# The second FFN product in 2x2 blocks: seven multiplications for sixteen of its twenty-two row tiles

## The chip, the cores and the metric

The kernel runs on one core of a Trainium2 chip. The core has a matrix engine (PE in the profile, its weight loads as PEld), a vector engine (DVE), an activation engine (ACT), a general-purpose engine (POOL), and a queue that only issues transfers (SP). Each works through a queue of its own in a fixed order; semaphores make one wait for another. The metric is device time of one execution in microseconds, the median of the runs.

## The reference

A decoder layer on 1024 tokens of width 1024: two kinds of attention, gates, an output projection, and then a SwiGLU FFN of inner width 2816 (22 row tiles of 128). All in float32. The part that changes is the last line but one:

```python
        h2 = rms_norm(x, norm_ffn_g[layer])
        gu = h2 @ w_ffn_in[layer]
        x = x + (jax.nn.silu(gu[..., :D_FF]) * gu[..., D_FF:]) @ w_ffn_down[layer]
    return rms_norm(x, norm_final_g)
```

Call `A` the 1024 x 2816 activation and `W` the 2816 x 1024 matrix `w_ffn_down`. The second product is `A @ W`, to which `x` (the residual) is added before the last norm.

## The kernel before, in words

Float32 products are made of three PE instructions each. `split` (L95 to L97) turns a float32 operand into a rounded part `hi` (a copy on ACT, L96) and the rest `lo` (a subtraction on DVE, L97: both inputs and the output lie in SBUF). `mm3` (L99 to L102) multiplies hi by hi, hi by lo and lo by hi into the same PSUM bank. One such instruction takes 128 rows of the left operand's 128 columns and 512 columns of the right one. There are six banks of the kind `pd` that this stage uses.

The first FFN product already runs in 2x2 blocks with seven multiplications: there `left_side` (L260 to L278) combines the weights' blocks on POOL (lines L272 to L277), and `up` (from L1013) makes 20 of the 22 row tiles of `A`, each of which POOL stores to `a_dram` (L1039).

The second product, which the change rewrites, is at the end. It walks over nine groups of row tiles (1, 1, 2, 3, 3, 2, 3, 3 and 4 of them). Of each row tile it loads 128 rows of `A` and 128 rows of `W` (`load_w`, L107 to L123; 512 KB each, issued by SP) and splits them. Then it goes through the eight token tiles and the two halves of the columns: one PSUM bank collects the group's products (3 per row tile), and DVE adds the bank to the accumulator `acc` in SBUF (L1080; in the first group ACT copies, L1078). In the fourth group POOL adds the residual to `acc` (L1086). In the last group each finished token tile is normed (L1081 to L1097) and stored by ACT and SP (L1099). Buffers for split rows are seven deep, so loads and splits run ahead of PE.

The order of the instructions in each engine's queue is made when the program is built: a scheduler goes by its own estimate of times. A place in a queue is fixed from then on.

Of the kernel before, what the change touches and what calls it, by code (L numbers as in the profile page):

```python
# [20 lines left out]
HALF = 512  # L21
# [9 lines left out]
NFF = DFF // P  # L31
# [16 lines left out]
def layer_kernel(  # L48
# [39 lines left out]
    def nm(s):  # L88
        uid[0] += 1
        return f"{s}_{uid[0]}"  # L90

    def pd():
        return psd.tile([P, HALF], F32, tag="d", name=nm("pd"))

    def split(hi, lo, src):  # L95
        nc.scalar.activation(out=hi, in_=src, func=AF.Copy)  # L96
        return nc.vector.tensor_tensor(out=lo, in0=src, in1=hi.bitcast(F32), op=ALU.subtract)  # L97

    def mm3(psum, w, m, start, stop):  # L99
        nc.tensor.matmul(psum, w.hi, m.hi, start=start, stop=False)  # L100
        nc.tensor.matmul(psum, w.hi, m.lo, start=False, stop=False)  # L101
        last_mm[0] = nc.tensor.matmul(psum, w.lo, m.hi, start=False, stop=stop)  # L102
# [31 lines left out]
    def load_gain(pool, g):  # L134
        t = pool.tile([P, D], F32, tag="gain", name=nm("gain"), bufs=1)
        nc.scalar.dma_start(out=t[:], in_=g.broadcast_to([P, D]))
        return t

# [243 lines left out]
    with pool_of("foxv", 2) as vpool:  # L382
# [31 lines left out]
        for i in range(NT):  # L414
            load_x()
            hh, c = divmod(i * P, HALF)
# [139 lines left out]
    fpool = f_ctx.__enter__()  # L556
# [286 lines left out]
    for i, (br, dt) in enumerate(merge_order):  # L843
        n = br * KT + dt
# [200 lines left out]
    h_ctx.__exit__(None, None, None)  # L1045


    groups, at = [], 0
    for n in (1, 1, 2, 3, 3, 2, 3, 3, 4):
        groups.append(list(range(at, at + n)))  # L1050
        at += n
    with pool_of("down", 1) as fpool:
        acc = fpool.tile([P, NT, D], F32, name="acc", bufs=1)
        for gi, grp in enumerate(groups):
            last = gi == len(groups) - 1
            if gi == 4:
                gainf = load_gain(fpool, norm_final_g.unsqueeze(0))
            ats, ws = [], []
            for j in grp:
                for to, src, tag in ((ats, a_dram[j], "at"), (ws, w_ffn_down[j * P:(j + 1) * P, :], "wd")):  # L1060
                    to.append(load_w(src, 1, D) if gi == 0 else
                              load_w(src, 1, D, tag=tag, bufs=7, pool=fpool, rbufs=2 if gi == 1 else 3,
                                     rpool=wpool if gi == 1 else fpool))
            for t in range(NT):
                sq = [None, None]
                if last:
                    xf = fpool.tile([P, D], F32, tag="xf", name=nm("xf"), bufs=3)
                if gi == 3:
                    xr = fpool.tile([P, D], F32, tag="xf", name=nm("xr"), bufs=3)
                    nc.gpsimd.dma_start(out=xr[:], in_=x1_dram[t])  # L1070
                for ch in range(2):
                    cs = slice(ch * HALF, (ch + 1) * HALF)
                    pt = pd()
                    for n in range(len(grp)):
                        mm3(pt[:], ats[n][:, 0, t * P:(t + 1) * P], ws[n][:, 0, cs],
                            n == 0, n == len(grp) - 1)
                    if gi == 0:
                        nc.scalar.activation(out=acc[:, t, cs], in_=pt[:], func=AF.Copy)  # L1078
                    else:
                        nc.vector.tensor_tensor(out=acc[:, t, cs], in0=pt[:], in1=acc[:, t, cs], op=ALU.add)  # L1080
                    if last:  # L1081
                        sq[ch] = small.tile([P, 1], F32, tag="sq", name=nm("sq"))
                        nc.scalar.activation(out=xf[:, cs], in_=acc[:, t, cs], func=AF.Square,
                                             accum_out=sq[ch][:])
                if gi == 3:
                    nc.gpsimd.tensor_tensor(out=acc[:, t], in0=acc[:, t], in1=xr[:], op=ALU.add)  # L1086
                if last:
                    ss = small.tile([P, 1], F32, tag="ss", name=nm("ss"))
                    nc.vector.tensor_tensor(out=ss[:], in0=sq[0][:], in1=sq[1][:], op=ALU.add)
                    nc.vector.tensor_tensor(out=xf[:], in0=acc[:, t, :], in1=gainf[:], op=ALU.mult)  # L1090
                    r = rstd(ss, True)
                    for ch in range(2):
                        cs = slice(ch * HALF, (ch + 1) * HALF)
                        if ch == 0:
                            nc.scalar.activation(out=xf[:, cs], in_=xf[:, cs], func=AF.Copy, scale=r[:, 0:1])
                        else:
                            nc.vector.tensor_scalar(out=xf[:, cs], in0=xf[:, cs], scalar1=r[:, 0:1],  # L1097
                                                    scalar2=None, op0=ALU.mult)
                        (nc.scalar, nc.sync)[ch].dma_start(out=out[t * P:(t + 1) * P, cs], in_=xf[:, cs])  # L1099


# [27 lines left out]
```

## Time and profile before

| what | value |
|---|---|
| median of three runs (lowest to highest) | 1507.62 us (1504.62 to 1509.13) |
| the profiled execution's own time | 1507.19 us |
| its span from first to last instruction | 1505.5 us |
| mean granted PE clock | 0.995 |
| PE busy over the span | 1463.1 us (97%) |
| first matmul of the second product | 1247.47 us |
| last matmul of the second product ends | 1497.45 us |
| matmuls of the second product | 1056 (22 row tiles x 16 banks x 3) |

Times in the views are microseconds from the span's start. A group's row gives how often, the busy time, the mean of one in ns, and the engine's idle time just before it with what ended it. A timeline's row gives start, length, engine, line, output<-inputs and shape. A busy PE share counts overlapping instructions, so the distance from one weight load to the next (PEld) is the better clock of PE's pace.

### The profile page before, as it was taken

The numbers are of one execution on the slowest core, as the hardware profiler recorded it, in microseconds if no ns is written. First come the engines' busy times: TensorE is split into PE (matmuls) and PEld (weight loads), VectorE is DVE, ScalarE is ACT, GpSimd is POOL, SyncE is SP. The second block draws the span as 40 slices with busy tenths as digits, with TensorE's granted clock in tenths as the row PEclk, the third lists the DMA queues.
The fourth block names the chain that finished last, engine by engine and source line by source line (L and its number), as shares of the span: only waits on it lengthen the run. The fifth ranks groups of instructions, "written<-read, shape, count | busy, mean of one in ns | idle before, by whom it ended". The sixth has DMA issues, their size and how long they took to land.

```text
span 1505.5 us, 18223 instructions
## 1 busy us (share of the span) xinstructions
PE 1463.1 (97%) x6920; PEld 1183.9 (79%) x6920; DVE 910.7 (60%) x1344; ACT 530.6 (35%) x808; POOL 440.8 (29%) x398
## 2 busy tenths in 40 slices
PE   6999999999999999999999999999999999999997
PEld 6898888886767666688888788888888877888886
DVE  6482654449888999736528944444444435856546
ACT  5242332226765332355215432222222225312113
POOL 1002434445443311100000245555555552240000
PEclk9999999999999999999999999999999999999999
DMA  8132454475453442175623132222222235643202
GB/s 253 43 105 70 137 165 124 137 202 122 131 137 117 141 165 71 52 238 168 227 64 133 42 91 66 82 84 84 84 84 84 84 99 197 205 144 90 93 14 98
DMA packets 148503, 177.91 MB, mean 118 GB/s; under 512 B 12096, under 2 KB 113472, under 8 KB 148416
## 3 DMA queue, kind: packets, MB, share of 16 engines
q1 hardware_dynamic: 115536, 97.56, 21.9%
q10 hardware_dynamic: 21264, 38.81, 8.1%
q0 software_dynamic: 11616, 40.39, 7.7%
q8 instruction: 54, 0.88, 0.2%
q14 instruction: 33, 0.27, 0.1%
HBM read 125.35 MB, written 51.38 MB: 117 GB/s over the span
## 4 chain that ended last, share of the span: by engine, by line
PE 84%; DVE 7%; DMA 3%; ACT 2%; issue 2%; POOL 2%; ACTq 0%; SPq 0%; DVEq 0%; POOLq 0%
PE pd L284 33%; PE pd L100 10%; PE pd L102 10%; PE pd L101 10%; PE pf L100 3%; PE pf L101 3%; PE pf L102 3%; PE pd L190 2%; PE pd L194 2%; PE pd L191 2%; PE pd L664 2%; PE pd L613 1%; PE pd L614 1%; DMA wr<-in_w_in_dram 1%; DVE mx L766 1%
## 5 line engine op out<-in xcount | busy, mean ns | idle before, releaser
L284 PE MATMUL pd<-hT_t,wh 128*128 128x512 f32 x856 | 264.4, 390 | 1.5 <-ACT cc L310 0.8
L96 ACT ACTIVATE wh<-wr 128x1024 fp32r<-128x1024 f32 (+2 forms) x152 | 139.4, 923 | 316.5 <-PE pd L101 88.8
L97 DVE TENSOR_TENSOR wl<-wr,wh 128x1024 fp32r<-128x1024 f32 (+2 forms) x152 | 164.3, 1084 | 132.3 <-ACT wh L96 132.0
L284 PE MATMUL pd<-tT,wh 128*128 128x512 f32 x768 | 236.3, 389 | 2.2 <-DVE v L952 1.1
L284 PEld LDWEIGHTS pd<-hT_t,wh 128*128 128x128 f32 x856 | 160.5, 188 | 35.3 <-ACT cc L310 1.2
L284 PEld LDWEIGHTS pd<-tT,wh 128*128 128x128 f32 x768 | 144.0, 188 | 32.9 <-DVE v L952 1.6
L284 PE MATMUL pd<-hT_t,wl 128*128 128x512 f32 x428 | 168.0, 393 | 0.2 <-DVE wl L97 0.2
L272 POOL TENSOR_TENSOR s<-wr 128x512 f32<-128x512 f32 x29 | 41.3, 1426 | 371.5 <-DVE tT L97 203.2
L284 PE MATMUL pd<-tT,wl 128*128 128x512 f32 x384 | 148.5, 390 | 0.1
L100 PE MATMUL pd<-wh,wh 128*128 128x512 f32 x352 | 137.3, 391 | 3.4 <-DVE acc L1080 2.0
L101 PE MATMUL pd<-wl,wh 128*128 128x512 f32 x352 | 137.0, 389 | 0.0
L102 PE MATMUL pd<-wh,wl 128*128 128x512 f32 x352 | 137.0, 389 | 0.0
L1080 DVE TENSOR_TENSOR acc<-pd,acc 128x512 f32<-128x512 f32 x128 | 85.4, 686 | 66.9 <-PE pd L102 66.8
L97 DVE TENSOR_TENSOR wl<-s,wh 128x1024 fp32r<-128x1024 f32 x58 | 73.8, 1274 | 68.8 <-ACT wh L96 68.8
L100 PE MATMUL pf<-hT_t,wh 128*128 128x512 f32 x288 | 114.3, 397 | 0.4 <-ACT wh L96 0.4
L101 PE MATMUL pf<-hT_t,wh 128*128 128x512 f32 x288 | 114.2, 397 | 0.0
L102 PE MATMUL pf<-hT_t,wl 128*128 128x512 f32 x288 | 113.6, 395 | 0.0
L96 ACT ACTIVATE wh<-s 128x1024 fp32r<-128x1024 f32 x58 | 61.4, 1060 | 132.3 <-POOL s L273 103.2
L284 PEld LDWEIGHTS pd<-hT_t,wl 128*128 128x128 f32 x428 | 80.3, 188 | 21.7 <-DVE wl L97 5.4
L284 PEld LDWEIGHTS pd<-tT,wl 128*128 128x128 f32 x384 | 72.1, 188 | 15.4 <-DVE wl L97 0.5
L100 PEld LDWEIGHTS pd<-wh,wh 128*128 128x128 f32 x352 | 66.1, 188 | 19.6 <-DVE acc L1080 2.9
L102 PE MATMUL pd<-wh,hT_t 128*128 128x512 f32 (+1 forms) x208 | 79.1, 382 | 0.0
(251 smaller groups left out, 2756.1 us busy)
## 6 DMA issues: line engine op xcount, KB each, us to landing
wr<-in_w_in_dram SPq DMA_DIRECT2D x46, 512.0 KB, 4.7
wr<-in_w_ffn_in_dram SPq DMA_DIRECT2D x44, 512.0 KB, 4.2
wr<-a_dram SPq DMA_DIRECT2D x22, 512.0 KB, 4.2
wr<-in_w_ffn_down_dram SPq DMA_DIRECT2D x22, 512.0 KB, 4.0
a_dram<-a POOLq DMA_DIRECT2D x20, 512.0 KB, 5.1
g_dram<-fst ACTq DMA_DIRECT2D x32, 256.0 KB, 2.3
land<-g_dram SPq DMA_DIRECT2D x16, 512.0 KB, 3.4
dqk_dram<-qo POOLq DMA_DIRECT2D x20, 256.0 KB, 3.7
```

Source lines behind the costliest of these rows:

```text
L96: nc.scalar.activation(out=hi, in_=src, func=AF.Copy)
L97: return nc.vector.tensor_tensor(out=lo, in0=src, in1=hi.bitcast(F32), op=ALU.subtract)
L100: nc.tensor.matmul(psum, w.hi, m.hi, start=start, stop=False)
L101: nc.tensor.matmul(psum, w.hi, m.lo, start=False, stop=False)
L102: last_mm[0] = nc.tensor.matmul(psum, w.lo, m.hi, start=False, stop=stop)
L190: nc.tensor.matmul(pt[hh][:], w.hi[:, k], m.hi, start=(k == 0), stop=False)
L191: nc.tensor.matmul(pt[hh][:], w.hi[:, k], m.lo, start=False, stop=False)
L194: nc.tensor.matmul(pt[hh][:], w.lo[:, k], m.hi, start=False, stop=(k == kt - 1))
L272: nc.gpsimd.tensor_tensor(out=s12[:, :4], in0=u1, in1=u2, op=ALU.add)
L284: last_mm[0] = nc.tensor.matmul(bank[:], p, q, start=first and k == 0 and n == 0, stop=k == 3 and n == 2, skip_group_check=True)
L664: nc.tensor.matmul(po[half[e], HALF - width[j]:], vf[j // 4][:, j % 4, pr, e], L[:, off[j]:off[j + 1]], start=(j == nj - 1), stop=(j == 0) ...
L1080: nc.vector.tensor_tensor(out=acc[:, t, cs], in0=pt[:], in1=acc[:, t, cs], op=ALU.add)
```

## The change

Row tiles 0, 1 and 2 are now done one by one as before (`PLAIN_UP`), and 19, 20 and 21 together at the end (`LAST`), where the norm is. The sixteen between are three chunks of 4, 6 and 6 row tiles. In a chunk of `2c` row tiles, `A`'s part is cut into four blocks (first or second half of the tokens, first or second `c` row tiles) and `W`'s part likewise (row tiles by halves of the columns). `block` makes seven products of such blocks instead of eight: four banks each, `c` row tiles deep, 12c matmuls. A chunk takes 84c matmuls where it took 96c.

The price is combined operands. Eight sums or differences of blocks per chunk (`comb`) run on POOL, each over 128 x (c*512) elements with both inputs in SBUF. Every product splits both of its operands anew (`product`): 14 splits of 128 x (c*512) per chunk, each a copy on ACT and a subtraction on DVE, where a chunk had 4c splits of 128 x 1024 before. Two partial sums belong to three quarters of the result: they are kept apart in `shared` over all chunks (`keep`), and only in the last chunk POOL adds them (`share`, four additions of 128 x 2048). The residual comes in the second chunk, in eight additions of 128 x 1024 on POOL. The raw rows of a chunk lie in four of five buffers of one tag; the temporaries `s1`, `s2`, `t1`, `t2` have one buffer each, and `gainf` now shares `t2`'s. In the last rows the multiplication by the gain is on POOL for token tiles 0 to 5. When a bank is added to `acc`, `acc` is now the first input and the bank the second.

```diff
-    for n in (1, 1, 2, 3, 3, 2, 3, 3, 4):
+    PLAIN_UP = ((0,), (1,), (2,))
+    CHUNKS = (range(3, 7), range(7, 13), range(13, 19))
+    LAST = range(19, NFF)
+    CM = max(len(c) for c in CHUNKS) // 2
...
+        shared = [fpool.tile([P, NT // 2, HALF], F32, name=nm("shared"), bufs=1) for _ in range(2)]
+        def op():
+            return fpool.tile([P, CM, HALF], F32R, tag="op", name=nm("op"), bufs=8)
+        def raw_rows():
+            return fpool.tile([P, CM, S], F32, tag="raw", name=nm("raw"), bufs=5)
...
+        def add(out, bank, op=ALU.add):
+            nc.vector.tensor_tensor(out=out, in0=out, in1=bank[:], op=op)
...
+            def comb(out, p, q, op=ALU.subtract):
+                nc.gpsimd.tensor_tensor(out=out, in0=p, in1=q, op=op)
+                return out
+            def product(p, q, banks):
+                ops = []
+                for src in (p, q):
+                    hi, lo = op()[:, :c], op()[:, :c]
+                    split(hi, lo, src)
+                    ops.append(Pair(hi, lo))
+                l, r = ops
+                new = banks is None
+                banks = banks or [pd() for _ in range(NT // 2)]
+                for t, bank in enumerate(banks):
+                    ts = slice(t * P, (t + 1) * P)
+                    for n in range(c):
+                        for k, (x_, y_) in enumerate(((l.hi, r.hi), (l.hi, r.lo), (l.lo, r.hi))):
+                            nc.tensor.matmul(bank[:], x_[:, n, ts], y_[:, n], start=new and n == 0 and k == 0,
+                                             stop=n == c - 1 and k == 2, skip_group_check=True)
+                return banks
...
+            banks = product(a11, b11, None)
+            keep(0, banks)
+            banks = product(a12, b21, banks)
+            into(0, 0, banks)
+            s1, s2, t1, t2 = [tmp(n) for n in ("s1", "s2", "t1", "t2")]
+            comb(s1, a21, a22, ALU.add)
+            comb(s2, s1, a11)
+            comb(t1, b12, b11)
+            comb(t2, b22, t1)
+            banks = product(s2, t2, None)
+            into(0, 1, banks, residual=False)
+            banks = product(comb(a21, a11, a21), comb(b12, b22, b12), banks)
+            keep(1, banks)
+            banks = product(s1, t1, None)
+            into(H, 1, banks)
+            banks = product(comb(a12, a12, s2), b22, banks)
+            into(0, 1, banks)
+            if last:
+                share(acc[:, :H, HALF:], 0)
+                share(shared[0][:], 1)
+                share(acc[:, H:, HALF:], 0)
+            banks = product(a22, comb(b21, t2, b21), None)
+            into(H, 0, banks, ALU.subtract)
+            if last:
+                share(acc[:, H:, :HALF], 0)
```

How the queues now stand, at three places. First POOL in the second product. Before, its only work there was the residual:

```order
L1086 TENSOR_TENSOR acc<-acc,xr_10007 128x1024
L1086 TENSOR_TENSOR acc<-acc,xr_10032 128x1024
L1070 DMA xr_10082<-x_dram 128x1024
L1070 DMA xr_10107<-x_dram 128x1024
L1086 TENSOR_TENSOR acc<-acc,xr_10057 128x1024
```

Now, at the third chunk (L1122 is `comb`, L1158 the residual of the second chunk, L1157 its load):

```order
L1122 TENSOR_TENSOR s_1601_10724<-s_1600_10723,raw_10607 128x1536
L1122 TENSOR_TENSOR raw_10607<-raw_10607 128x3x512
L1158 TENSOR_TENSOR acc<-acc,xr_10487 128x2x512
L1158 TENSOR_TENSOR acc<-acc,xr_10490 128x2x512
L1157 DMA xr_10542<-x_dram 128x2x512
L1157 DMA xr_10545<-x_dram 128x2x512
L1122 TENSOR_TENSOR t_1603_10726<-raw_10619,t_1602_10725 128x1536
L1122 TENSOR_TENSOR raw_10611<-raw_10619,raw_10611 128x3x512
L1158 TENSOR_TENSOR acc<-acc,xr_10542 128x2x512
L1158 TENSOR_TENSOR acc<-acc,xr_10545 128x2x512
L1122 TENSOR_TENSOR raw_10615<-raw_10615,s_1601_10724 128x3x512
```

Six of the eight residual additions have thus moved in among the third chunk's combinations. The chunks' combinations stand eight in a row before that (second chunk), and the four additions of `share` and the six gain multiplications (L1209) stand in a row behind.

Second, DVE at one product of the second chunk (L97 is a split's subtraction, L1099 the addition of a bank):

```order
L97 TENSOR_TENSOR op_10388<-raw_10203,op_10387 128x1536
L1099 TENSOR_TENSOR acc<-acc,pd_10341 128x512
L97 TENSOR_TENSOR op_10392<-raw_10207,op_10391 128x1536
L1099 TENSOR_TENSOR acc<-acc,pd_10342 128x512
L1099 TENSOR_TENSOR acc<-acc,pd_10343 128x512
L1099 TENSOR_TENSOR acc<-acc,pd_10344 128x512
```

Every product has this pattern: one split, one bank, one split, three banks. Before, DVE had up to thirteen banks in a row between two splits.

Third, ACT at the third chunk (L96 is a split's copy, L136 the load of the last norm's gain):

```order
L96 ACTIVATE op_10735<-t_1603_10726 128x1536
L136 DMA gain_10991<-in_norm_final_g_dram 128x1024
L96 ACTIVATE op_10785<-raw_10607 128x1536
L96 ACTIVATE op_10789<-raw_10611 128x1536
```

The gain's load waits until POOL has read `t2` for the last time (the chunk's last combination), and the copies for the fourth product now stand behind it.

More of the change, by code (lines that the diff above doesn't have):

```diff
@@ new lines, in rows, with whole @@
+        def rows(j):
+            return a_dram[j], w_ffn_down[j * P:(j + 1) * P, :]
+        def whole(j, own):
+            if own:
+                return [load_w(src, 1, D)[:, 0] for src in rows(j)]
+            raw, both = raw_rows(), []
+            for i, src in enumerate(rows(j)):
+                load(raw[:, i], src)
+                hi, lo = [t[:].rearrange("p a c -> p (a c)")[:, :S] for t in (op(), op())]
+                split(hi, lo, raw[:, i])
+                both.append(Pair(hi, lo))
+            return both
@@ L1071, in layer_kernel, with plain_rows @@
+        def plain_rows(js, own, evac):
+            both = [whole(j, i == own) for i, j in enumerate(js)]
+            for t in range(NT):
                 for ch in range(2):
@@ L1073, in layer_kernel @@
                     pt = pd()
[L1074 to L1078, printed above, removed]
-                    else:
[L1080 to L1099, printed above, removed]
+                    for n, (a, w) in enumerate(both):
+                        mm3(pt[:], a[:, t * P:(t + 1) * P], w[:, cs], n == 0, n == len(both) - 1)
@@ new lines, in plain_rows, with first_rows, more_rows, block @@
+                    evac(t, ch, acc[:, t, cs], pt)
+        def add(out, bank, op=ALU.add):
+            nc.vector.tensor_tensor(out=out, in0=out, in1=bank[:], op=op)
+        def first_rows(t, ch, out, pt):
+            nc.scalar.activation(out=out, in_=pt[:], func=AF.Copy)
+        def more_rows(t, ch, out, pt):
+            add(out, pt)
+        def block(js, first, last):
+            c = len(js) // 2
+            raws = []
+            for part in (js[:c], js[c:]):
+                for i in range(2):
+                    raw = raw_rows()
+                    for n, j in enumerate(part):
+                        load(raw[:, n], rows(j)[i])
+                    raws.append((raw[:, :c, :HALF], raw[:, :c, HALF:]))
+            (a11, a21), (b11, b12), (a12, a22), (b21, b22) = raws
+            def tmp(n):
+                return fpool.tile([P, CM, HALF], F32, tag=n, name=nm(n), bufs=1)[:, :c]
+            def comb(out, p, q, op=ALU.subtract):
[17 more added lines that the diff above has]
+                return banks
+            def keep(n, banks):
+                for t, bank in enumerate(banks):
+                    if first:
+                        nc.scalar.activation(out=shared[n][:, t], in_=bank[:], func=AF.Copy)
+                    else:
+                        add(shared[n][:, t], bank)
+            def into(t0, ch, banks, op=ALU.add, residual=js == CHUNKS[1]):
+                cs = slice(ch * HALF, (ch + 1) * HALF)
+                for t, bank in enumerate(banks):
+                    add(acc[:, t0 + t, cs], bank, op)
+                for t in range(t0, t0 + NT // 2, 2) if residual else ():
+                    xr = wpool.tile([P, 2, HALF], F32, tag="wr", name=nm("xr"), bufs=2)
+                    nc.gpsimd.dma_start(out=xr[:], in_=x1_dram[t:t + 2, :, cs].rearrange("t p c -> p t c"))
+                    nc.gpsimd.tensor_tensor(out=acc[:, t:t + 2, cs], in0=acc[:, t:t + 2, cs], in1=xr[:], op=ALU.add)
+            def share(out, n):
+                nc.gpsimd.tensor_tensor(out=out, in0=out, in1=shared[n][:], op=ALU.add)
+            H = NT // 2
+            banks = product(a11, b11, None)
[23 more added lines that the diff above has]
+                share(acc[:, H:, :HALF], 0)
```

58 lines of the change are left out of this document (37 added, 21 removed).

## The prediction

> **What bounds the kernel now.** I read the page first, for the busiest engine and the chain, then the windows, waits and weight loads of the second product.
>
> ```profile
> PE 1463.1 (97%) x6920; PEld 1183.9 (79%) x6920; DVE 910.7 (60%) x1344; ACT 530.6 (35%) x808; POOL 440.8 (29%) x398
> PE 84%; DVE 7%; DMA 3%; ACT 2%; issue 2%; POOL 2%; ACTq 0%; SPq 0%; DVEq 0%; POOLq 0%
> 1300.00:1480.00 180.00, 180.00 (x796) 149.10 (x795) 104.54 (x151) 37.53 (x53) 22.87 (x13) 1.00 0.31 97
> PE pd L100 <- DVE acc L1080: 2.0, 1, 2.0
> PE pd L100 <- ACT acc L1078: 1.1, 3, 0.5
> PE pd L100 <- DVE gt L952: 0.2, 1, 0.2
> 1299.86 0.19 PEld L100 LDWEIGHTS pd<-wh,wh 128*128 128x128 f32 x1
> ...
> 1305.98 0.19 PEld L100 LDWEIGHTS pd<-wh,wh 128*128 128x128 f32 x1
> ```
>
> The chain is PE for 84% of the span. In the long window of the second product (columns after the length: PE, PEld, DVE, ACT, POOL, clock, DMA share) PE has no idle time at full clock, while DVE works 104.54 of 180 us and POOL 22.87. The waits of PE in the whole second product come to 3.3 us. Between the two weight loads shown lie 27 steps: 6.12 / 27 = 0.2267 us per matmul. So PE bounds this stage, and fewer matmuls shorten it as long as the others keep up.
>
> **What is removed.** Three chunks drop 12c matmuls each with c = 2, 3, 3: 96 of 1056. 96 x 0.2267 = **-21.8 us**. The matmuls left have the same shape, so I keep their pace.
>
> **What is added**, with its durations:
>
> ```profile
> L1080 DVE TENSOR_TENSOR acc<-pd,acc 128x512 f32<-128x512 f32 x128 | 85.4, 686 | 66.9 <-PE pd L102 66.8
> L97 DVE TENSOR_TENSOR wl<-wr,wh x152: 414/1217/3416, 10.6 to 1431.6; 128x1024 fp32r<-128x1024 f32 x107, 128x512 fp32r<-128x512 f32 x37, 128x256 fp32r<-128x256 f32 x8
> L97 DVE TENSOR_TENSOR tT<-f,tT x11: 1215/1220/2282, 89.6 to 856.7; 128x1024 fp32r<-128x1024 f32 x8, 128x2048 fp32r<-128x2048 f32 x3
> L277 POOL TENSOR_TENSOR s<-wr,s 128x512 f32<-128x512 f32 x20 | 25.7, 1286 | 0.2
> L1086 POOL TENSOR_TENSOR acc<-acc,xr x8: 2387/2400/3299, 1308.0 to 1335.7; 128x1024 f32<-128x1024 f32 x8
> ```
>
> A split's subtraction on DVE takes 1.22 us at 1024 elements and 2.28 at 2048, so 1.75 at the 1536 of a c = 3 chunk (an estimate halfway). POOL takes 1.29 at 512 and 2.40 at 1024: 1.11 more per 512, so 3.51 at 1536 and 4.62 at 2048 (estimates; the strided forms have no row).
>
> Each by itself fits. A product of c = 3 is 36 matmuls, 8.16 us; DVE's two splits and four banks are 2 x 1.75 + 4 x 0.60 = 5.9 us (banks in a row follow each other every 0.60: 1.27 for two, below). POOL's 8 x 3.51 = 28.1 us fit into seven products, 57.1 us. By these sums alone the gain would stay. But DVE and POOL do not run side by side:
>
> ```profile
> 1333.79 1.23 DVE L97 TENSOR_TENSOR wl<-wr,wh 128x1024 fp32r<-128x1024 f32 x1 [0.85 <-ACT wh L96]
> 1335.53 4.55 DVE L97 TENSOR_TENSOR wl<-wr,wh 128x1024 fp32r<-128x1024 f32 x2
> 1335.70 3.30 POOL L1086 TENSOR_TENSOR acc<-acc,xr 128x1024 f32<-128x1024 f32 x1 [2.31 <-DVE acc L1080]
> 1225.71 1.22 DVE L97 TENSOR_TENSOR wl<-s,wh 128x1024 fp32r<-128x1024 f32 x1
> 1225.79 2.28 POOL L1037 TENSOR_TENSOR sg<-gt,sg 128x512 f32<-128x512 f32 x1 [1.73 <-ACT sg L1036]
> 1311.37 1.27 DVE L1080 TENSOR_TENSOR acc<-pd,acc 128x512 f32<-128x512 f32 x2
> 1312.13 2.39 POOL L1086 TENSOR_TENSOR acc<-acc,xr 128x1024 f32<-128x1024 f32 x1 [1.76 <-DVE acc L1080]
> ```
>
> At 1335.70 POOL starts while a split runs on DVE (1335.53 to 1336.75): its addition takes 3.30 us instead of 2.40 and ends at 1339.00, 2.25 after that split. The second split, right behind the first, takes 3.42 (the 3416 of the row above) and ends at 1340.08, 1.08 after POOL. They take turns, each waiting out the whole of the other's instruction. The same at 1225.71, where POOL's 1.29 become 2.28. A bank's addition, which has one input in PSUM, disturbs nothing (1311.37 against 1312.13). The kernel before hardly meets this in the second product, with eight POOL additions; the change brings 24 combinations, eight residual additions, four of `share` and six gain multiplications against 54 splits.
>
> [...]
>
> So in turn a split costs 1.09 us (1024) or 1.62 (1536), an addition 2.27, 3.38 or 4.49 us: each 0.13 less than alone. POOL's rows in the order follow each other almost without waits for DVE, so wherever POOL has work, each split waits out one POOL instruction, and DVE's banks (one or three between splits, 0.6 to 1.8 us) fit under it. PE has six banks and a product takes four, so a product that is split late stops PE. What PE loses, place by place:
>
> - Start, rows 0 to 2: as before, 0 (-2 to +2).
> - First chunk (c = 2): PE needs 5.44 us a product, two turns take 2 x (1.09 + 2.27) = 6.72, which loses 1.28 for each of at most four products, 5.1; POOL starts under the rows before, so 0 at best. I take **+2.5**.
> - Second chunk's eight combinations: `t1` has one buffer, so POOL begins them after the first chunk's fifth product. They meet the splits of that chunk's last two products, 2 x (2 x (1.09 + 3.38) - 5.44) = 7.0, and of two of their own, 2 x (2 x (1.62 + 3.38) - 8.16) = 3.7. **+10.7**, nearer the upper end, because eight stand in a row (0 if all fall beside banks; with the 16 banks of four products not hidden, 9.6 more).
> - Third chunk: eight combinations and the six residual additions among them are 14, as many as its splits: 8 x 5.00 + 6 x (1.62 + 2.27) = 63.3 against 57.1: **+6.2** (0, or +23.0 with 28 banks not hidden).
> - `share`: four POOL additions of 4.49 meet the four splits of rows 20 and 21, 4 x (1.09 + 4.49) = 22.3 us. Meanwhile PE has the third chunk's last product (8.16) and some 30 matmuls of the last rows that need none of these (6.8): **+7.3** (0 to 10).
> - ACT: the gain's load waits for the third chunk's last combination, and the copies for its fourth product stand behind; with POOL late, about half of one POOL instruction: **+2** (0 to 3.5).
> - Tail:
>
> ```profile
> 1496.76 5.30 SPq L1099 DMA_DIRECT2D out_dram<-xf  x2
> 1497.06 0.39 PE L102 MATMUL pd<-wh,wl 128*128 128x512 f32 x1
> 1501.96 0.34 ACTq L1099 DMA_DIRECT2D out_dram<-xf  x1
> ```
>
> Now 8.05 us pass from the last matmul's end (1497.45) to the end (1505.5), with one token tile behind it; the stores of two tiles lie 5 us apart. After `share` POOL still owes six multiplications of 2.40; with 4 x 4.62 before them that is 32.9 us, about the 32.6 us of the last rows' 144 matmuls. Tile 5 then ends beside the last matmul, and tiles 6 and 7 queue behind it on DVE: **+5** (0 to +8).
>
> What costs nothing: ACT's 14 copies of some 1.5 us, 21 in 57, and the extra bank additions, 5.9 of 8.16 us with the splits. If DVE had no such slack, each product would pay the difference.
>
> Sum: -21.8 + 2.5 + 10.7 + 6.2 + 7.3 + 2 + 5 = **+11.9 us**. The profiled execution took 1507.19 (span 1505.5 and 1.7 around it); 1519.1. The median stands 0.4 above it: **1519.5 us**. The terms' ends put 1508 to 1538 around it.
>
> **The rivals.**
>
> *The turns cost PE nothing* (faster). Combinations fall beside banks, and PE's spare banks take the rest: 1507.6 - 21.8 + 3 for the tail = 1489. For it: 5.9 of 8.16 us, and PE waited 2.0 us for DVE in the whole stage before. Against: the 3416 ns row, and pieces that are now half as long again. Chance 0.20.
>
> *The turns cost half* (no change). Half of each term above is 17, less 21.8: 1503; three quarters, 25.3, give 1511. Between them lies no change. Chance 0.07, of it 0.06 within the bound.
>
> *The banks take turns too* (slower still). Now `acc` is the first input and PSUM the second; before it was the other way round, and no row shows this order beside POOL. If it counts like two SBUF inputs, nothing hides under POOL: 9.6 + 16.8 for chunks two and three, and some 4 at the end: 1550. [...] Chance 0.07. It decides from the first bank that runs over 1 us.
>
> That the change does not do what it says is ruled out by the order: 960 matmuls stand where 1056 stood. Late transfers are the smallest risk:
>
> ```profile
> wr<-a_dram SPq DMA_DIRECT2D x22, 512.0 KB, 4.2
> ```
>
> A c = 3 chunk needs twelve of these in 57 us, but only four of five buffers hold a chunk, so each waits for a combined block's split; I count it in the range.
>
> **How the numbers follow.** Forecast 0.66, within 1508 to 1538. With the rivals: faster by over 0.3% (4.5 us, about what a measurement of this kernel can tell from none) 0.20 + 0.01 = 0.21; within 0.06; slower 0.66 + 0.07 = 0.73. The range of 8 in 10 reaches down to 1497, toward the faster case whose centre stays outside, and up to 1538.
>
> **What would show it.** DVE's L97 at 1536 elements: near 1.75 us where nothing meets, many at 3 to 5; POOL's L1122 likewise, 3.5 alone and 5 beside a split. Matmul waits for DVE: some 25 us over the stage, most at products' starts around the second chunk's beginning and at the last rows. Last matmul to end: 13 us. If L97 stays near 1.75 throughout, or PE's waits are under 10 us, the forecast is wrong; if L1099 runs over 1 us, the third rival holds.

## The result and the profile after

The changed kernel took **1522.88 us** (median of 4 runs, 1520.11 to 1524.25), the kernel before 1506.45 us beside it (4 runs, 1504.62 to 1509.13): ratio 1.0105, 95% interval 1.0083 to 1.0128. It is slower by about 16 us. Its profiled execution took 1523.45 us, with a span of 1521.3.

The page of the kernel after: the engines, the chain, and the long window of the second product (columns as before: length, PE, PEld, DVE, ACT, POOL, clock, DMA share, GB/s).

```profile
PE 1452.9 (96%) x6824; PEld 1170.3 (77%) x6824; DVE 983.1 (65%) x1344; ACT 554.9 (36%) x826; POOL 575.1 (38%) x432
PE 67%; DVE 13%; POOL 6%; DMA 5%; issue 4%; ACT 4%; POOLq 0%; ACTq 0%; SPq 0%; DVEq 0%
1300.00:1480.00 180.00, 161.67 (x671) 130.12 (x670) 161.77 (x119) 56.34 (x46) 120.40 (x35) 0.95 0.29 100
```

96 matmuls fewer are there. PE's share of the chain fell from 84 to 67%, and DVE's and POOL's rose. In the window where PE had no idle time it now has 18.3 us, DVE went from 104.54 to 161.77 us busy, and the mean clock is 0.95. What PE waited for from 1245 to the end (us in total, times, longest):

```profile
PE pd L1139 <- DVE op L97: 11.1, 7, 2.8
PE pd L101 <- DVE op L97: 5.1, 2, 3.0
PE pd L1139 <- DVE acc L1099: 4.3, 1, 4.3
PE pd L100 <- DVE acc L1099: 1.7, 1, 1.7
```

With two small rows these are 22.9 us, against 3.3 before. The groups of the same stretch (count | busy, mean ns) tell why (what a split waits after its start counts as busy: the one at 1318.35 below, of 1024 elements, lasts 3.90 us, the shortest of that size 1.21):

```profile
L97 DVE TENSOR_TENSOR op<-raw,op 128x1536 fp32r<-128x1536 f32 x20 | 58.8, 2942 | 9.3 <-ACT op L96 9.3
L97 DVE TENSOR_TENSOR op<-raw,op 128x1024 fp32r<-128x1024 f32 x18 | 47.9, 2676 | 9.4 <-ACT op L96 9.4
L1099 DVE TENSOR_TENSOR acc<-acc,pd 128x512 f32<-128x512 f32 x108 | 68.4, 676 | 4.0 <-PE pd L1139 2.9 <-PE pd L102 1.1
L1122 POOL TENSOR_TENSOR raw<-raw,raw 128x1536 f32<-128x1536 f32 x2 | 10.0, 5004 | 0.0
L1122 POOL TENSOR_TENSOR t<-raw 128x1536 f32<-128x1536 f32 x2 | 7.0, 3511 | 17.6 <-DMA raw<-in_w_ffn_down_dram 11.2 <-DVE op L97 6.4
```

A split of 1536 elements takes 2.94 us on average where 1.75 were estimated for it alone, POOL's combination 3.5 alone and 5.0 beside splits, and a bank's addition 0.676, as before. One such meeting in the timeline, at the start of the second chunk's combinations:

```profile
1317.00 4.16 POOL L1122 TENSOR_TENSOR s<-raw,raw 128x1536 f32<-128x1536 f32 x1 [0.26 <-DMA raw<-a_dram]
1321.24 4.34 POOL L1122 TENSOR_TENSOR s<-s,raw 128x1536 f32<-128x1536 f32 x1
...
1318.35 3.90 DVE L97 TENSOR_TENSOR op<-raw,op 128x1024 fp32r<-128x1024 f32 x1
1322.17 1.87 DVE L1099 TENSOR_TENSOR acc<-acc,pd 128x512 f32<-128x512 f32 x3
...
1322.30 7.75 PE L1139 MATMUL pd<-op,op 128*128 128x512 f32 x26 [2.78 <-DVE op L97]
```

The split begins at 1318.35 under a POOL combination that ends at 1321.16, and ends 1.09 us after that. The matmuls that need it start at 1322.30 after a wait of 2.78 us, and here begins the first cost that the prediction did not have:

```profile
1322.00:1324.00 2.00, 1.70 (x4) 1.41 (x5) 2.00 (x5) 0.00 (x0) 2.00 (x1) 0.56 0.00 0
1324.00:1326.00 2.00, 2.00 (x6) 1.54 (x6) 2.00 (x2) 0.00 (x0) 2.00 (x2) 0.59 0.00 0
1340.00:1342.00 2.00, 2.00 (x6) 1.52 (x6) 2.00 (x3) 0.00 (x0) 2.00 (x1) 0.50 0.00 0
1434.00:1436.00 2.00, 2.00 (x6) 1.60 (x5) 2.00 (x2) 0.74 (x1) 0.69 (x1) 0.50 0.83 238
1436.00:1438.00 2.00, 2.00 (x6) 1.53 (x5) 2.00 (x3) 0.00 (x0) 0.00 (x0) 0.50 0.66 254
1474.00:1476.00 2.00, 2.00 (x6) 1.54 (x5) 2.00 (x2) 0.00 (x0) 2.00 (x1) 0.54 0.00 0
```

After the waits of 2.4, 2.8, 3.0 and 4.3 us PE is granted half its clock, for 3.4 us each time and for 6.8 us after the longest: six matmuls in 2 us instead of nine or ten. By these windows (busy time times what is missing of the clock) the four cost 1.6, 1.7, 1.7 and 2.9 us, 8 us in all.

### The profile page after: what moved, and what is told of

It reads as the page before. It is cut to its first block, busy times and chain, and to the rows that moved or that the text cites. A ratio compares the mean times of both kernels' runs of the same rounds, so it can differ in the third digit from the quotient of the medians.

```text
span 1521.3 us, 18058 instructions
## 1 busy us (share of the span) xinstructions
PE 1452.9 (96%) x6824; PEld 1170.3 (77%) x6824; DVE 983.1 (65%) x1344; ACT 554.9 (36%) x826; POOL 575.1 (38%) x432
## 4 chain that ended last, share of the span: by engine, by line
PE 67%; DVE 13%; POOL 6%; DMA 5%; issue 4%; ACT 4%; POOLq 0%; ACTq 0%; SPq 0%; DVEq 0%
PE pd L284 27%; PE pd L100 5%; PE pd L101 5%; PE pd L102 5%; PE pd L1139 4%; PE pf L100 3%; PE pf L101 3%; PE pf L102 3%; DVE op L97 3%; DMA wr<-in_w_ffn_in_dram 2%; PE pd L190 2%; PE pd L194 2%; PE pd L191 2%; ACT wh L96 2%; POOL sg L1037 2%
## 5 line engine op out<-in xcount | busy, mean ns | idle before, releaser
L97 DVE TENSOR_TENSOR wl<-wr,wh 128x1024 fp32r<-128x1024 f32 (+2 forms) x112 | 113.3, 1012 | 118.8 <-ACT wh L96 118.5
L1139 PE MATMUL pd<-op,op 128*128 128x512 f32 x672 | 160.7, 401 | 15.3 <-DVE op L97 11.1
L96 ACT ACTIVATE wh<-wr 128x1024 fp32r<-128x1024 f32 (+2 forms) x112 | 97.6, 872 | 203.2 <-DMA wr<-in_w_ffn_in_dram 51.0
L1139 PEld LDWEIGHTS pd<-op,op 128*128 128x128 f32 x672 | 129.7, 194 | 46.2 <-DVE op L97 14.1
L97 DVE TENSOR_TENSOR wl<-s,wh 128x1024 fp32r<-128x1024 f32 x58 | 73.8, 1273 | 71.5 <-ACT wh L96 68.6
L97 DVE TENSOR_TENSOR op<-raw,op 128x1536 fp32r<-128x1536 f32 (+1 forms) x38 | 106.8, 2816 | 18.6 <-ACT op L96 18.6
L96 ACT ACTIVATE wh<-s 128x1024 fp32r<-128x1024 f32 x58 | 61.3, 1059 | 132.9 <-POOL s L273 104.8
L96 ACT ACTIVATE op<-raw 128x1536 fp32r<-128x1536 f32 (+1 forms) x38 | 47.4, 1286 | 99.7 <-PE pd L1139 60.8
L101 PE MATMUL pd<-wl,hT_t 128*128 128x512 f32 (+1 forms) x208 | 78.9, 380 | 0.2 <-DVE wl L97 0.2
## 6 DMA issues: line engine op xcount, KB each, us to landing
g_dram<-fst ACTq DMA_DIRECT2D x32, 256.0 KB, 2.3
dqk_dram<-qo POOLq DMA_DIRECT2D x20, 256.0 KB, 3.7
```

What stands on the lines that cost most here:

```text
L1139: nc.tensor.matmul(bank[:], x_[:, n, ts], y_[:, n], start=new and n == 0 and k == 0, stop=n == c - 1 and k == 2, skip_group_check=True)
```

## The ledger, and what had to be tested

From the first matmul of the second product to the end of its last one ("the stage") passed 250.15 us before (1247.30 to 1497.45; the table of the kernel before has 1247.47 for the first matmul, where the trace has 1247.30) and 258.25 after (1249.66 to 1507.91); from there to the end ("the tail") 8.05 and 13.39. How late each place is follows from the starts of the products: what lies between the start of one and that of the next, less 24 or 36 times 0.2267:

| place | predicted | measured |
|---|---|---|
| ahead of the stage | 0 | +2.4 |
| 96 matmuls | -21.8 | -21.8 |
| rows 0 to 2 | 0 | -1.0 |
| first chunk, products 1 to 5 | +2.5 | 0 |
| second chunk's combinations: products 6 and 7 of the first chunk, 1 and 2 of the second (4.6, 1.4, 4.2, 1.3) | +10.7 | +11.5 |
| third chunk's combinations and the residual: product 7 of the second (1.4), product 2 of the third (1.9) | +6.2 | +3.3 |
| third chunk, product 4 (the ACT queue) | +2 | +8.6 |
| `share` and rows 20, 21 | +7.3 | +7.3 |
| tail | +5 | +5.3 |
| sum | +11.9 | +15.6 of 15.8 |

The first row is taken for scatter of single executions: over the runs below the stage begins between 1246.6 and 1250.8, without relation to their edits; of the kernel before there is one trace. So stages and tails are compared from here on, beside the medians.

A ledger says where time is lost, not why. The theory: DVE's splits and POOL's additions take turns in reading SBUF. The rivals: POOL is simply late with the sums (not so for the second chunk's row: its four products read raw rows, or sums that POOL had finished by 1302.03, 20 us before the first of these waits ends); DVE is simply full; and, for the large row of product 4, the gain's load on ACT. The runs:

| run | median us | ratio to before (95%) | stage | tail |
|---|---|---|---|---|
| kernel after | 1522.88 | 1.0105 (1.0083 to 1.0128) | 258.3 | 13.4 |
| kinds | 1512.39 (one run) | | 248.3 | 13.3 |
| fills | 1500.98 | 0.9945 (0.9926 to 0.9964) | 237.3 | 12.5 |
| split_psum | 1492.14 | 0.9887 (0.9871 to 0.9903) | 227.6 | 14.2 |
| split_psum_gain | 1488.82 | 0.9865 (0.9848 to 0.9882) | 227.5 | 9.1 |
| comb_dve | 1522.77 | 1.0091 (1.0075 to 1.0108) | 258.0 | 12.0 |
| share_dve | 1515.42 | 1.0036 (1.0025 to 1.0048) | 249.8 | 14.2 |
| gain_late | 1517.37 | 1.0052 (1.0037 to 1.0067) | 257.4 | 8.4 |
| gain_sync | 1521.16 | 1.0080 (1.0057 to 1.0103) | 257.1 | 13.5 |
| no_residual | 1518.35 | 1.0066 (1.0045 to 1.0086) | 256.6 | 11.9 |
| no_residual_gain_sync | 1518.90 | 1.0069 (1.0054 to 1.0084) | 256.0 | 13.3 |

The kernel before took 1506.45 us beside the kernel after and 1508.0 to 1510.1 beside the other runs, so the ratios are what compares. Each edit is made to the kernel after.

## Which POOL instructions take turns: kinds

```diff
-                nc.gpsimd.tensor_tensor(out=out, in0=p, in1=q, op=op)
+                if ncomb[0] < 8 or k in (0, 5):
+                    nc.gpsimd.tensor_tensor(out=out, in0=p, in1=q, op=op)
+                elif k in (1, 6):
+                    for _ in range(3):
+                        nc.gpsimd.memset(out, 0.5)
...
+                        nc.gpsimd.tensor_scalar(out=out, in0=p, scalar1=0.5, scalar2=None, op0=ALU.mult)
```

`k` is the combination's number in its chunk, 0 to 7; the first eight are the first chunk's.

> The combinations of the first chunk stay. In the second and third chunk two of eight stay as they are (the first and the sixth, two inputs); the others are replaced by POOL instructions of other kinds on the same tiles, repeated so that POOL stays as busy: fills without an input, selects and copies and scalings with one input. The sums are therefore not formed and the values are not the reference's; loads, splits, products and waits stand where they stood. This run is read by L97's and POOL's durations where they overlap, not by its time. Theory (turns need two inputs in SBUF on both sides): L97 at 1536 takes 1.75 us beside fills, selects, copies and scalings and 3 to 5 us only beside the additions that are left; the others show one duration each. Rival (every POOL instruction that touches SBUF takes turns with a split): L97 exceeds 1.75 us beside all kinds, by what is left of the POOL instruction, and those rows spread too. In the trace of the kernel before, the 64 selects of 128x128 at L620 took 620 ns on average and one at L574 284, which speaks for the rival.

Rows of DVE and POOL from this run's timeline, a fill first, then a scaling with one input:

```profile
1343.48 1.39 POOL L1130 MEMSET raw<- 128x1536 f32 x1
1343.94 1.76 DVE L97 TENSOR_TENSOR op<-s,op 128x1536 fp32r<-128x1536 f32 x1
...
1378.37 4.10 POOL L1140 TENSOR_SCALAR raw<-raw 128x1536 f32<-128x1536 f32 x1
1378.76 4.45 DVE L97 TENSOR_TENSOR op<-raw,op 128x1536 fp32r<-128x1536 f32 x1
1382.44 2.10 POOL L1133 TENSOR_SCALAR_AFFINE_SELECT t<-raw 128x1536 f32<-128x1536 f32 x1
```

Neither theory stands as written. All 12 fills took 1.37 to 1.40 us, and a split beside one took 1.76. But one input was enough to take turns: beside the scaling the split lasted 4.45 us and ended 0.74 after it, and the select behind it took 2.10 and ended 1.33 after that split (another select of the same shape, at 1375.38, took 3.01 and ended 1.35 after the split it met). So in these rows what counted on POOL's side was whether the instruction read SBUF: the scaling and the selects did, the fills only wrote it.

## Turns or lateness: fills

Since the fills took no turns (1.37 to 1.40 us, and the split beside one 1.76), POOL can be kept as busy without them:

```diff
-                nc.gpsimd.tensor_tensor(out=out, in0=p, in1=q, op=op)
+                if ncomb[0] < 8:
+                    nc.gpsimd.tensor_tensor(out=out, in0=p, in1=q, op=op)
+                else:
+                    nc.gpsimd.tensor_tensor(out=out[:, :, :1], in0=p[:, :, :1], in1=q[:, :, :1], op=op)
+                    for _ in range(3):
+                        nc.gpsimd.memset(out, 0.5)
```

> In the second and third chunk each combination on POOL becomes a subtraction of three elements a partition (which keeps its waits) and three fills of its output, 3 x 1.38 = 4.1 us as long as the fills of the run before lasted, so that POOL is as busy and as late as with combinations of 3.5 to 5.0 us. The sums are not formed and the values are not the reference's. The first chunk's combinations, the residual's and the shared sums' additions stay. Theory (the combinations cost PE time only by taking turns with the splits; a fill took none): of the changed kernel's extra time the 11.6 us at the second chunk's start and about 2 of the third chunk's go; some 13 us less, 1509 where the changed kernel has 1522.9, or 1 to 4 us above the kernel before. Rival (products start late because POOL delivers the sums late, in whatever way it spends the time): the waits stay, 13 to 16 us above the kernel before.

PE's waits for DVE in the second product of this run:

```profile
PE pd L101 <- DVE op L97: 5.1, 2, 3.0
PE pd L100 <- DVE acc L1099: 1.6, 1, 1.6
PE pd L1147 <- DVE op L97: 0.3, 1, 0.3
```

From the second chunk's first combination until the third chunk's combinations and the residual are done, POOL was busy for 92.94 of 103.2 us (1312.6 to 1415.8), in the kernel after for 99.09 of 121.5 (1313.2 to 1434.7). Yet of the products' waits 0.3 us is left; only those of rows 20 and 21, where the shared sums stand, are as they were. The stage is 20.9 us shorter, more than the 13 expected: product 4's 8.6 us went too. So the rival of lateness falls for the second and third chunk's combinations. For product 4 alone this run does not decide: its last subtraction reads `t2` ahead of its fills, and the gain's load went at 1404.31, 16.5 us after the third chunk's first product had begun, where it went 25.4 us after it in the kernel after.

## The turns taken away, with the sums kept: split_psum and split_psum_gain

Bank additions, with one input in PSUM, never waited: all 108 to `acc` in the kernel after took 0.67 to 0.69 us. Two PSUM banks stand unused in this stage, so a split can be made to look the same:

```diff
-                    split(hi, lo, src)
+                    nc.scalar.activation(out=hi, in_=src, func=AF.Copy)
+                    for n in range(c):
+                        part = psf.tile([P, HALF], F32, tag="f", name=nm("pf"))
+                        nc.scalar.activation(out=part[:], in_=src[:, n], func=AF.Copy)
+                        nc.vector.tensor_tensor(out=lo[:, n], in0=part[:], in1=hi[:, n].bitcast(F32), op=ALU.subtract)
```

and likewise in `whole`, by halves of a row; only rows 0 and 19, two splits each, keep the old form.

> Only the splits of the blocks and of the raw rows change: ACT also copies the value, 512 elements at a time, into one of two PSUM banks that stand unused in this stage, and DVE forms the low half from that bank and the high half in SBUF. The sums, POOL's work, the matmuls and the results are the same. DVE gets three pieces of about 0.6 us for one of 1.75, ACT some 3 x 0.6 us more for each split: 2 x (1.5 + 1.8) = 6.6 of 8.16 us a product. Theory (only instructions of which both read SBUF take turns; bank additions of 0.68 us never did): the low halves no longer wait for POOL, POOL's additions fall to 3.5 and 4.6 us, PE's waits of 22.9 us fall to some 5, and the stage from the first matmul of the second product to the last falls from 258 to 229 to 233 us, with the tail as it was at 13 us: 9 to 14 us below the kernel before, ratio 0.991 to 0.994. Rival (DVE and ACT are simply too full, or POOL's sums are late whatever DVE does): ACT has twice its work and the products wait for its copies instead, no gain over the changed kernel, 10 to 20 us above the kernel before.

The groups of the new split and of a combination, PE's waits, and the window from 1300 to 1470:

```profile
L1139 DVE TENSOR_TENSOR op<-pf,op 128x512 fp32r<-128x512 f32 x112 | 73.9, 684 | 20.2 <-ACT pf L1138 13.6 <-ACT op L1135 6.5
L1127 POOL TENSOR_TENSOR raw<-raw,raw 128x1536 f32<-128x1536 f32 x2 | 7.1, 3538 | 0.0
...
PE pd L100 <- ACT acc L1107: 0.9, 3, 0.3
PE pd L100 <- DVE acc L1104: 0.2, 1, 0.2
PE pd L100 <- DVE gt L952: 0.2, 1, 0.2
...
1300.00:1470.00 170.00, 169.90 (x749) 140.16 (x748) 134.68 (x225) 125.82 (x182) 106.94 (x38) 1.00 0.32 115
```

The same combinations take 3.54 us, where the kernel after had up to 5.0, and PE waits 1.3 us in all, at full clock. The stage is 227.6 us, 22.6 below the kernel before, where 96 matmuls are worth 21.8. So all that the stage lost, some 30 us, hung on the turns: on the waits, on POOL's lateness that came of them, and on the low clock behind them. ACT went from 56.34 to 125.82 us busy in that window and held nobody up. The ratio of 0.9887 is below the forecast 0.991 to 0.994, because PE's waits fell to 1.3 us and not to some 5.

split_psum_gain adds the edit of gain_late (below).

> The splits through PSUM of the run before, and in the last rows the gain and the scale in one step on DVE, as in gain_late. Theory: both effects add, since they lie in different stretches: the stage 229 to 233 us, the tail 8.0 to 8.5 us instead of 13.4, which is 14 to 19 us below the kernel before, ratio 0.987 to 0.991. Rival (with the stage shorter, DVE gets behind in the last rows): the tail stays at 12 to 14 us, ratio 0.991 to 0.994.

Stage 227.5, tail 9.1 instead of 14.2: both effects add in stretches of their own. The stage is shorter than the forecast 229 to 233 us and the tail a little longer than 8.0 to 8.5. With 0.9865 it is the fastest of these versions, 1.35% (1.18 to 1.52) below the kernel before.

## The obvious remedy: comb_dve

```diff
-                nc.gpsimd.tensor_tensor(out=out, in0=p, in1=q, op=op)
+                nc.vector.tensor_tensor(out=out, in0=p, in1=q, op=op)
```

> All 24 combinations run on DVE instead of POOL; shared sums, residual and gain stay. A combination of 1536 elements then costs DVE about 1.75 us as a split does, and cannot meet one. By sums: 14 x 1.75 + 28 x 0.60 + 8 x 1.75 = 55.3 us of DVE in a chunk of 57.1 us of PE, so that DVE alone would nearly keep up, and the time would fall by the second and third chunk's terms, 12 to 15 us, to 1508 to 1511 where the changed kernel has 1522.9. By order: four to eight combinations stand one behind the other in DVE's queue, 7 to 14 us in which no bank is added, and PE has six banks, so the waits only move: 1520 to 1530. I hold the second likelier, because DVE takes its instructions in order.

No better than the kernel after (1.0091), as the second reading forecast, but not for its reason. In the timeline one or two combinations stand in a row, never four to eight; DVE is nearly full (columns as above):

```profile
1300.00:1470.00 170.00, 158.27 (x673) 127.48 (x671) 157.86 (x134) 61.45 (x54) 40.42 (x17) 0.98 0.30 106
```

157.86 of 170 us, with the residual's and the shared sums' turns still in it. The waits are more and shorter (19.4 us in all, the longest 3.0). Some come earlier: from row 1's first matmul to the first chunk's, 30.9 us pass instead of 24.2, and the first chunk's combinations now stand among the banks of rows 1 and 2.

## Single terms: share_dve, gain_late, gain_sync, no_residual

**`share`.** The four additions of the shared sums on DVE instead of POOL:

```diff
-                nc.gpsimd.tensor_tensor(out=out, in0=out, in1=shared[n][:], op=ALU.add)
+                nc.vector.tensor_tensor(out=out, in0=out, in1=shared[n][:], op=ALU.add)
```

> The four additions of the shared sums run on DVE instead of POOL. The ledger of the changed kernel's trace gives 7.3 us to them (two waits of PE for L97 of rows 20 and 21, 3.0 and 2.1 us, and matmuls at half pace after the first). Theory (POOL's 4.6 to 5.5 us additions hold up those splits): the splits fall back to about 1.2 us, DVE pays 4 x 2.3 = 9.1 us instead, which fits beside 30 free matmuls and the last product, and the time falls by about 7 to 1516 (1512 to 1519). Rival (the last rows are late for another reason, or DVE has no room for 9.1 us more): no change, 1520 to 1526.

```profile
L97 DVE TENSOR_TENSOR op<-raw,op 128x1024 fp32r<-128x1024 f32 x4 | 4.7, 1217 | 0.0
L1161 DVE TENSOR_TENSOR acc<-acc,shared 128x2048 f32<-128x2048 f32 x3 | 6.9, 2284 | 0.0
```

The splits of rows 20 and 21 fell to 1.22 us and both waits are gone; the stage is 8.4 us shorter, 7.3 expected. The tail stays.

**Tail.** Gain and scale in one step on DVE, nothing on POOL:

```diff
-            (nc.gpsimd if t < NT - 2 else nc.vector).tensor_tensor(out=xf[:], in0=acc[:, t, :], in1=gainf[:],
-                                                                   op=ALU.mult)
...
+                nc.vector.scalar_tensor_tensor(out=xf[:, cs], in0=acc[:, t, cs], scalar=r[:, 0:1], in1=gainf[:, cs],
+                                               op0=ALU.mult, op1=ALU.mult)
```

> In the last rows the gain and the scale are multiplied in one step on DVE (two halves of 512 elements a token tile) after the row's scale is known, instead of a multiplication by the gain on POOL (six tiles) or DVE (two) and a scaling by ACT and DVE. POOL then has nothing to do in the last rows. Theory (the tail's extra 5 us are POOL's multiplications, for which DVE's tiny sum at L1208 and the scaling at L1217 wait: 871 and 728 ns on average, against 160 and 487 before): the time from the last matmul to the end falls from 13.4 to about 8 to 9 us, and the time to about 1518 (1516 to 1520). Rival (the tail is long because the last rows start behind `share` and DVE is full): DVE gets one pass more of 1.2 us a tile, and the tail stays at 13 us or grows.

The sum of two numbers a partition in the kernel after, then here:

```profile
L1208 DVE TENSOR_TENSOR ss<-sq,sq 128x1 f32<-128x1 f32 x8 | 7.0, 871 | 1.3 <-ACT xf L1204 1.2
```
```profile
L1208 DVE TENSOR_TENSOR ss<-sq,sq 128x1 f32<-128x1 f32 x8 | 1.3, 156 | 0.4 <-ACT xf L1204 0.3
```

Even a sum of one element a partition waited for POOL's multiplication: three of the eight took 1.56 to 2.35 us. So did a scaling with only one tensor as input, which takes 0.48 us elsewhere; the last row shows DVE waiting for POOL in the plain way, for the tile that it is to scale:

```profile
1492.31 2.40 POOL L1209 TENSOR_TENSOR xf<-acc,gain 128x1024 f32<-128x1024 f32 x1 [1.75 <-ACT xf L1204]
1492.54 2.45 DVE L1217 TENSOR_SCALAR xf<-xf,r 128x512 f32<-128x512 f32 x1
...
1509.60 0.48 DVE L1217 TENSOR_SCALAR xf<-xf,r 128x512 f32<-128x512 f32 x1 [0.73 <-POOL xf L1209]
```

At 1509.60, 1.7 us after the last matmul, the last three banks still stood behind that scaling. gain_late takes both kinds of waiting away and does not tell them apart. Tail 8.4 instead of 13.4; the rival falls.

**Product 4 of the third chunk.** In the kernel after, ACT, POOL and PE around it:

```profile
1422.01 3.51 POOL L1122 TENSOR_TENSOR raw<-t,raw 128x1536 f32<-128x1536 f32 x1
...
1425.55 0.34 ACTq L136 DMA_DIRECT2D gain<-in_norm_final_g_dram  x1
1425.94 2.86 ACT L96 ACTIVATE op<-raw 128x1536 fp32r<-128x1536 f32 x2 [14.76 <-POOL raw L1122]
...
1430.92 0.47 PE L1139 MATMUL pd<-op,op 128*128 128x512 f32 x1 [4.27 <-DVE acc L1099]
```

gain_sync issues that load from SP's queue:

```diff
-        gainf = load_gain(fpool, norm_final_g.unsqueeze(0), "t2")
+        gainf = fpool.tile([P, D], F32, tag="t2", name=nm("gain"), bufs=1)
+        nc.sync.dma_start(out=gainf[:], in_=norm_final_g.unsqueeze(0).broadcast_to([P, D]))
```

> The gain's load is issued from SP's queue instead of ACT's; everything else stays. In the changed kernel's trace ACT issues it at 1425.55, right after POOL's last combination, and the two copies for the third chunk's fourth product stand behind it; that product starts 5.9 us late and its first matmuls run at half pace, 8.5 us in all. Theory A (the gain's load alone holds these copies): 8 us less, 1515 (1512 to 1518). Theory B (a row of the last rows is next in line: its copy on ACT and its split on DVE stand before the same product's bank additions, and its load waits for a buffer that the residual's addition on POOL frees at about 1430): the wait only changes its name, 1520 to 1525.

```profile
1416.48 2.87 ACT L96 ACTIVATE op<-raw 128x1536 fp32r<-128x1536 f32 x2 [7.10 <-PE pd L1139]
1432.60 1.06 ACT L96 ACTIVATE wh<-wr 128x1024 fp32r<-128x1024 f32 x1 [13.25 <-DMA wr<-a_dram]
...
1428.40 0.33 SPq L119 DMA_DIRECT2D wr<-a_dram  x1
...
1425.19 3.19 POOL L1158 TENSOR_TENSOR acc<-acc,xr 128x1024 f32<-128x1024 f32 x1
...
1435.56 1.65 PE L1139 MATMUL pd<-op,op 128*128 128x512 f32 x3 [5.22 <-DVE acc L1099]
```

The copies moved from 1425.94 to 1416.48, and PE waits all the same, two banks further on: a row of the last rows is next in ACT's and DVE's queues, its load could only go at 1428.40, when a residual addition on POOL (to 1428.38) freed the buffer. The stage is 1.2 us shorter. Theory A falls.

Then the residual was left out, alone and with the gain's load moved:

```diff
-                for t in range(t0, t0 + NT // 2, 2) if residual else ():
...
-                    nc.gpsimd.tensor_tensor(out=acc[:, t:t + 2, cs], in0=acc[:, t:t + 2, cs], in1=xr[:], op=ALU.add)
```

> The residual is left out: its eight loads and its eight additions on POOL, so the values are not the reference's. The gain's load stays in ACT's queue behind the last combination, everything else stays. To be read at the third chunk's fourth product, which the changed kernel started 5.9 us late, with matmuls at half pace after it, 8.5 us in all; the first products are expected to be ordered a little differently. Theory C (POOL is late there because four residual additions of 2.4 to 3.9 us stand among the third chunk's combinations; the gain's load and the last rows' buffers only pass the lateness on): POOL finishes the last combination some 10 us earlier, no wait at that product, 8 us less there, and up to 4 us lost at the start where POOL's earlier combinations meet more splits: 1514 to 1519. Theory A (the gain's load on ACT itself): the wait stays as it was, 1520 to 1523.

> The residual left out as in no_residual, and the gain's load issued from SP's queue as in gain_sync. By theory C the second edit adds nothing to the first, within 1.5 us; by theory A only this one shows the gain of 8 us at the third chunk's fourth product.

In both the wait at product 4 is gone, and the second edit adds nothing to the first (1.0066 and 1.0069): theory C. The median of no_residual, 1518.35 us, lies in that theory's range. But the stage is only 1.6 and 2.2 us shorter, not 4 to 8: POOL, earlier now, met splits elsewhere: no_residual has waits of 1.8 us at the start, with half clock behind it, of 3.3 at an earlier product, and of 3.7 instead of 2.1 for the later of rows 20 and 21. While the turns stood, a hold-up taken away at one place came back at another.

## Why the prediction was right, step by step

The forecast of 1519.5 us, slower, came true at 1522.9, and by its own cause: PE was free of the 96 matmuls at an unchanged 0.2267 us each, and lost more than that to turns between DVE and POOL. The runs show the cause: with the turns gone and all else kept the stage ends 0.8 us better than the matmuls alone promise.

- **The three rivals.** Turns at no cost to PE, and at half cost (17 us by the prediction's terms), fall with 29.9 us lost in the stage and 5.3 in the tail. The waits of 22.9 us are near the 25 that were expected. That banks take turns too falls with 108 additions at 676 ns.
- **Second chunk, `share`, tail** (10.7, 7.3, 5) measured 11.5, 7.3 and 5.3, the last two tested by runs of their own. The first holds 3.3 us of half clock and `share` 1.7; without these the waits are smaller than I had them. That the tail would lengthen because `share` delays POOL was wrong: with `share` on DVE it was 14.2. It is POOL's multiplications themselves, which DVE met in turns and waited for.
- **First chunk** (+2.5, measured 0): six of its eight combinations ran before its first product (1291.93), the other two beside its products at no cost (1295.44 to 1302.03), which was the lower end. **Third chunk** (+6.2, measured 3.3): the sum counted six residual additions among the combinations. In POOL's queue only four stand between them (from 1390.80 and from 1408.53, two each), two come before and two behind; with four, the same sum gives 55.6 us, less than PE's 57.1. That two products start late all the same shows that adding up a chunk does not say where a turn falls.
- **The ACT term** (+2, range 0 to 3.5, measured 8.6) is the step that failed in size. I priced half a POOL instruction. ACT stood 14.8 us for POOL there, because four residual additions stand between the third chunk's combinations; and behind the copies stood a row whose load hung on a further residual addition. The queue was named rightly, its depth not.
- **Not in the sum at all:** half clock after waits, 8 us of the 29.9 that the stage lost. It lies inside the measured terms and made up for waits that were priced too high. That the sum came so near is in part luck: the first and third chunk's terms together were 5.4 us too high and ACT's 6.6 too low. The range of 1508 to 1538 is a judgement; the terms' ends, added up, give 1484 to 1558.
- **Left over:** +2.4 us ahead of the stage, taken for scatter; the medians differ by 16.4, as the profiled executions do by 15.8 in span.

## What to carry to other kernels

Before work goes to an idle POOL, count what DVE does meanwhile: here DVE's splits and POOL's instructions that read SBUF waited out each other (a split of 1.75 us took 4.45 beside a POOL scaling, a POOL combination of 3.5 us up to 5.0 beside splits; a DVE scaling with one tensor input took 2.45 instead of 0.48), so busy shares of 65 and 38% went with 22.9 us of waits of PE. Moving that work to DVE helped where DVE had room for it (`share`, a stage 8.4 us shorter) and not where it was nearly full (comb_dve, 157.86 of 170 us); putting one operand of DVE's instruction in PSUM, with a copy by an engine that had time (here ACT), took these turns away: combinations at 3.54 us, 1.3 us of waits. And when a stall is priced, follow the queue to its end and add what PE loses in clock behind it.

## What the runs showed of the hardware that was not expected

- Half clock followed short waits of PE, and where they fell mattered. In the traces of the kernels before and after it lasts 3.41 or 6.83 us up to the last matmul, and its starts lie on a grid of 3.413 us: in the kernel after 1322.22, 1339.29, 1431.45 and 1472.41, which are 5, 27 and 12 steps apart. In these two traces, from 40 us to the last matmul, it followed each of the eight steps at full clock in which PE idled 2.12 us or more (2.12 to 2.94), and none in which it idled 1.90 us or less. In no_residual 1.78 us within one step were followed by it (the wait before 1276.09; clock 0.50 from 1278 to 1280), so the runs show no sharp limit. A wait across the end of a step is split: 3.3 us before 1405.02 in no_residual, about 1.65 on either side if the steps are counted from its half clock at 1277.1, left the clock at 1.00, and so did 2.1 us before 1482.87 in the kernel after, of which 1.90 fell into one step.
- One input was enough on POOL's side (a scaling of 4.10 us beside a split of 4.45), an instruction with none did no harm: a fill of 1.39 us beside a split of 1.76.
- A DVE sum of 128x1 elements waited for POOL as a split did: 871 ns on average against 156. So did a scaling of 512 elements with one tensor input: 2.45 us against 0.48.
- A split in three pieces through PSUM cost DVE hardly more than in one: pieces of 684 ns that follow each other every 0.60 us, some 1.8 us, against 1.75 for 1536 elements.
